# The low part of a weight sum, by VectorE's subtraction or by a DMA that adds onto the negated high part

## The chip, the cores and the metric

The kernel runs on one core of a Trainium2 chip. The core has TensorE for matrix products (PE in the profile, its weight loads PEld), VectorE (DVE) and ScalarE (ACT) for elementwise work, GpSimd (POOL) and SyncE (SP). Each engine runs its own queue of instructions in order and waits on semaphores for the others. In the kernel before, all DMAs are issued from SP's queue. The metric is the device time of one execution in microseconds, the median over runs.

## The reference, cut to what matters

The model is a trunk of two layers, each of four sublayers on 512 tokens of 1024 features: a feed-forward block, a mixer (DeltaNet in the first layer, a state-space mixer in the second), cross-attention on a memory, and a second feed-forward block. There are thus four feed-forward blocks. Each is

```python
def swiglu(x, w_in, w_out):
    gate, up = jnp.split(x @ w_in, 2, axis=-1)
    return (jax.nn.silu(gate) * up) @ w_out

u = swiglu(rms_norm(h, g[0, 0]), ffn_w_in[l, 0], ffn_w_out[l, 0])
h = h + MACARON_W * rms_norm(u, g[0, 1])
```

with 1024 features in, 2816 hidden features (22 blocks of 128) and float32 throughout.

## The kernel before

**Two parts.** TensorE is given its operands as float32r, a rounded float32. To keep the accuracy, each operand is held as a high part (the value rounded, by a ScalarE copy into a float32r tile) and a low part (value minus high part, by a VectorE subtraction). A product then takes three matmuls, high by high, high by low and low by high; `mm3` (L141 to L145) issues them, L143, L144 and L145 in the profile. `weights` (L117) loads a tile of 128 x 1024 weights from HBM into `raw` and makes the two parts at L129 and L130; `split` (L133) does the same for a tile that is in SBUF already, high part at L137, low part at L138. The parts come from two rings, `whi` and `wlo`, of five buffers each, which the weights of all products share; `raw` has three buffers.

**The feed-forward stage.** The class FFN runs through the 22 hidden blocks; for each, one tile of gate weights g and one of up weights u is loaded. Blocks 0 and 1 are done by `plain`, the other 20 by `pair`, which replaces eight products of halves by seven (halves of the tokens, of the rows, and gate and up). For that it needs four sums of weight halves, made by VectorE at L485 to L489, a and b being the two halves of 512 columns:

```python
        sub(T1, u[:, a], g[:, a])
        sub(T2, u[:, b], T1)
        sub(T4, T2, g[:, b])
        w14 = t.split(self.T14)
        sub(T3, u[:, b], u[:, a])
        w23 = t.split(self.T23)
```

T1 and T4 are the halves of the tile T14, T2 and T3 those of T23. Each of the two tiles has one buffer only, in the place of the residual stream h, which lies in DRAM meanwhile; the profile calls them `h`. So T1 of the next pair may be written only when the split of T14 of this pair has read it, and T2 and T3 of the next pair only after the split of T23.

The seven products of a pair go to PSUM in the order of the code: two of g (tile `X`), one of T23's first half (`V`, the bank called ps_f), one of the second half of u itself, whose parts are made at L492 and L493 (`Z`, against S4), two of T14 (`Y`), one of T23's second half (`Z`, against S3). S2, S3 and S4 are sums of quarters of the normalised rows, made when the stage is entered. L502 to L513 combine the results, apply SiLU and put the hidden block into two parts (L468, L469).

After most pairs follows a slice of the output products (`slices`, PSUM banks s and c): the hidden blocks done so far against one tile of output weights. `rest` issues one after pair n when enough hidden blocks are there; by its list there is none after pairs 5, 7 and 9.

**Order.** The order of the instructions on each engine is laid out ahead of the run, by a priority that follows the order of the code, by what is ready, and by offsets in the table LATER. Semaphores and the reuse of buffers follow from what each instruction reads and writes. An instruction waits in its engine's queue and holds up all behind it.

Of the kernel before, what the change touches and what calls it, by code (L numbers as in the profile page):

```python
# [61 lines left out]
class Trunk:  # L62
# [39 lines left out]
    @contextmanager  # L102
    def later(self, n):
        """what is traced here gives way to the next n instructions"""
        n = LATER.get(n, 0)
        self.tc.cur_priority += n
        yield
        self.tc.cur_priority -= n
# [4 lines left out]
    def bank(self, tag):  # L113
        """a PSUM bank: a for the long products, f, s and c for the mixers' chains"""
        return self.pm.tile([P, T], F32, name="ps_" + tag, tag=tag, bufs={"a": 3, "f": 1}.get(tag, 2))

    def weights(self, src, pool=None, nt=4):  # L117
        """a tile of weights in two float32r parts that add up to it"""
        nc = self.nc
        n = src.shape[1]  # L120
        raw = self.wp.tile([P, D], F32, name="raw", tag="raw", bufs=3)
        if pool is None:
            hi = self.wp.tile([P, D], F32R, name="whi", tag="whi", bufs=5)
            lo = self.wp.tile([P, D], F32R, name="wlo", tag="wlo", bufs=5)
        else:
            hi = pool.tile([P, D], F32R, name="thi", tag="thi", bufs=nt)
            lo = pool.tile([P, D], F32R, name="tlo", tag="tlo", bufs=nt)
        nc.sync.dma_start(out=raw[:, :n], in_=src)
        nc.scalar.copy(hi[:, :n], raw[:, :n])  # L129
        nc.vector.tensor_sub(lo[:, :n], raw[:, :n], hi[:, :n])  # L130
        return hi, lo

    def split(self, raw):  # L133
# [5 lines left out]
        return hi, lo  # L139

    def mm3(self, ps, lhs, rhs, first, last):  # L141
        mm = self.nc.tensor.matmul
        mm(ps, lhs[0], rhs[0], start=first, stop=False)  # L143
        mm(ps, lhs[0], rhs[1], start=False, stop=False)  # L144
        mm(ps, lhs[1], rhs[0], start=False, stop=last)  # L145
# [6 lines left out]
    def heads(self, srcs, half, st, outer=False):  # L152
        """the first products of a phase, for half of the tokens, block by block of the rows as they come"""
        if half == 0:
            st["w"] = [self.weights(x) for x in srcs]
            st["ps"] = [self.bank(x) for x in "aaaf"]
        s = slice(half * 256, half * 256 + 256)
        n = range(len(srcs))
        with self.later(0 if half else 'head'):
            for k, i in [(k, i) for i in n for k in range(KB)] if outer else [(k, i) for k in range(KB) for i in n]:  # L160
                kk = slice(k * P, k * P + P)
                w, ps = st["w"][i], st["ps"][i]
                self.mm3(ps[:, s], (w[0][:, kk], w[1][:, kk]), (self.xh[:, k, s], self.xl[:, k, s]),
                         k == 0, k == KB - 1)

    def out_weights(self, src, fh, pool=None, nt=4):
        """[[hi, lo] of each block of 128 rows] for 512 output columns"""
        res = []
        for kp in range(src.shape[1]):
            hi, lo = self.weights(src[fh, kp], pool, nt)  # L170
            for n in range(2):
                ns = slice(n * T, n * T + T)
                res.append((hi[:, ns], lo[:, ns]))
        return res

    def out(self, xs, ws, i, fh, first, last, tag):
        """u[tokens of tile i, columns of half fh] (+)= xs^T ws"""
        ps = self.bank(tag)
# [19 lines left out]
    def rcol(self, ss):  # L198
        """(mean of the squares + eps) ** -0.5, from the two sums of 512 squares"""
        nc = self.nc  # L200
# [6 lines left out]
    def warm(self, func, x):  # L207
        """the tables of func, loaded when x is there"""
        w = self.nt.tile([P, 1], F32, name="warm")
        self.nc.scalar.activation(w, x, func)  # L210
# [8 lines left out]
    def post(self, i, square):  # L219
        """h += u * rsqrt(mean(u^2) + eps) * gain, and the sums of the squares of h"""  # L220
        nc = self.nc
# [13 lines left out]
    def features(self, src, ss, g, hi, lo, ts, tag="c"):  # L235
        """the normalised rows of src [tokens, 1024], transposed, times gain g, in two parts"""
        nc = self.nc
# [29 lines left out]
    def last_group(self, name, og, inner, ctx):  # L267
        """the last rows of a mixer's output projection, for the tail"""
        inner.close()
        pool = ctx.enter_context(self.tc.tile_pool(name="tw", bufs=2, reuse_waits="tile"))  # L270
        return [og[12 + k] for k in range(4)], self.tail_weights(self.ap[name][3], pool, 2)
# [9 lines left out]
    def conv(self, ps, dst, w):  # L281
        """causal taps along the tokens"""
        nc = self.nc
# [5 lines left out]
    def small_proj(self, name, pool, tag, bufs):  # L289
        """the 32 columns of per-head values, [32, tokens]"""  # L290
        nc = self.nc
# [9 lines left out]
    def rsqrt(self, pool, x, shape):  # L301
        """(x) ** -0.5 elementwise by Newton steps on a float32 guess; x is a small [P, n] view."""
        nc = self.nc
# [11 lines left out]
    def softplus(self, pool, x, shape):  # L315
        """log1p(exp(x)) in place, as max(x, 0) + 2 atanh(e / (e + 2)) with e = exp(-|x|)."""
        nc = self.nc
# [17 lines left out]
class FFN:  # L335
    """the input projection by seven products of halves (of the tokens, of the rows, gate and up) for eight"""
    spill = True
# [20 lines left out]
    def sums(self):  # L358
        """place for three sums of quarters of the normalised rows, in two parts"""
        self.sp = ExitStack()  # L360
# [5 lines left out]
    def enter(self, i, ss, tag):  # L366
        """the normalised rows of tile i, and for the later half of the tokens the sums of quarters, in two parts"""
        t, nc = self.t, self.t.nc
# [37 lines left out]
    def product(self, ps, w, x, first=True, last=True):  # L406
        """ps[feature, token] (+)= w^T x over four blocks of rows"""
        for k in range(4):
# [3 lines left out]
    def early(self, n, ws, tags):  # L412
        """the first half of the tokens of a pair, by plain products"""
        ps = []
# [30 lines left out]
    def plain(self, n):  # L445
        """a pair of hidden blocks by eight products; the later half of the tokens from the sums of its quarters"""
        t, nc = self.t, self.t.nc
# [25 lines left out]
    def pair(self, n):  # L473
# [13 lines left out]
        sub(T4, T2, g[:, b])  # L487
        w14 = t.split(self.T14)
        sub(T3, u[:, b], u[:, a])  # L489
        w23 = t.split(self.T23)  # L490
        b22 = [self.ip.tile([P, T], F32R, name="b" + x) for x in "hl"]
# [24 lines left out]
    def slices(self, gi):  # L516
        """the output products of a group of hidden blocks, two blocks at a time"""
        t, nc = self.t, self.t.nc
# [41 lines left out]
class DeltaNet:  # L560
# [29 lines left out]
    def rows(self, d):  # L590
        """[row][head, chunk][column] of the 8 matrices of a pair of heads in DRAM"""
        return d.rearrange("(e x) -> e x", e=8)[:, 0:P * P].rearrange("e (i j) -> i e j", j=P)

    def diag(self, d):
        """[head, chunk, block][row][column] of their diagonal blocks"""
        return bass.AP(d.tensor, d.offset, [[self.EC // 8, 64], [P, BS], [1, BS]])
# [18 lines left out]
    def gates(self):  # L615
        """beta, the decays' sums and what the state needs of them, per token and head."""
        t, nc, d1 = self.t, self.t.nc, self.d1
# [104 lines left out]
    def blocks(self, p):  # L722
        """the diagonal blocks of 16 of I + A inverted, by substitution, a block per partition"""
        nc = self.t.nc
# [13 lines left out]
    def solve(self, p, st):  # L738
        """U = transpose of (I + A)^-1, by doubling the diagonal blocks that are inverted."""
        t, nc, dp = self.t, self.t.nc, self.dp  # L740
# [424 lines left out]
class CrossAttention:  # L1165
# [21 lines left out]
    def memory(self):  # L1187
        """the normalised memory, in the place of half of the tokens"""
        t, nc, l = self.t, self.t.nc, self.l
# [10 lines left out]
    def keys_values(self):  # L1200
        """keys [feature, slot] and values [slot, feature] of the normalised memory, to DRAM."""
        t, nc, l = self.t, self.t.nc, self.l
# [105 lines left out]
def pack_out(w, sizes):  # L1308
    """per group of row blocks: [column half][pair of row blocks][128][2 * 512]"""
    res, k0 = [], 0  # L1310
# [11 lines left out]
def pack_z(w):  # L1322
    """[1024, 2048] -> per group of 256 columns two tiles of four row blocks"""
    return np.ascontiguousarray(w.reshape(2, 4, P, 8, 256).transpose(3, 0, 2, 1, 4)).reshape(8, 2, P, 1024)
# [113 lines left out]
```

## Time and profile before

| | us |
|---|---|
| median of 3 runs | 2842.75 |
| lowest and highest | 2831.45, 2849.64 |
| span of the profiled execution | 2839.1 |

The span goes from the first to the last instruction of one profiled execution; that execution's own device time is not among the three runs, which are others. The mean granted TensorE clock in it is 0.993 of full speed.

How to read the lines that the prediction shows: a line of groups gives the line of the code, the engine, the operation, output and input by the tiles' names, the shape and the count; behind the first bar the busy time in all and the mean of one in ns, behind the second the idle time of the engine just before and what ended it. A line of a stretch gives its bounds, its length, and for each engine the busy time with the number of instructions, then the granted clock, the busy share of the DMA engines and GB/s. A line of the timeline gives start and duration of an instruction in us. A line of DMA issues gives the count, the size of one and the median time from issue to landing.

The four feed-forward stages lie at about 0 to 350, 1100 to 1480, 1480 to 1840 and 2450 to 2839 us; their loops over the hidden blocks are the four stretches in the prediction.

### The profile page before, as it was taken

What the parts mean: (1) busy time and instruction counts of PE and PEld (TensorE: products, weight loads), DVE (VectorE), ACT (ScalarE), POOL (GpSimd) and SP (SyncE); (2) the same over time, 40 slices, a digit from 0 to 9 for tenths busy, and PEclk for the clock granted to TensorE, in tenths of its full rate; (3) what the DMA queues carried; (4) which work ended last, traced back from release to release, by engine and by line L of the source; (5) the groups of instructions that cost most, each with busy time, mean ns of one, the idle gap of its engine ahead of it and who ended that gap; (6) DMA issues with size and microseconds to landing.
All of it is one profiled execution on the core that took longest, in us unless ns stands there. A gap on an engine that the chain in (4) does not pass through costs nothing.

```text
span 2839.1 us, 46420 instructions
## 1 busy us (share of the span) xinstructions
PE 2791.8 (98%) x18032; PEld 2476.0 (87%) x18032; DVE 2076.1 (73%) x4057; ACT 1520.4 (54%) x2835; POOL 128.6 (5%) x141
## 2 busy tenths in 40 slices
PE   8999999999999999999999999999999999999998
PEld 7999987788878887999988999888888888799997
DVE  8887777666666565887778877777766766588776
ACT  5444486756475574544355443575554656454433
POOL 0000001000000000000000000012221200000000
PEclk9999999999999999999999999999999999999999
DMA  6333433232323532332343333433233363233233
GB/s 222 98 105 109 154 120 94 62 106 77 92 77 115 177 113 81 127 112 90 112 149 127 98 104 97 146 118 104 91 97 111 100 211 117 77 113 112 90 111 104
DMA packets 125916, 320.76 MB, mean 113 GB/s; under 512 B 27472, under 2 KB 46672, under 8 KB 125184
## 3 DMA queue, kind: packets, MB, share of 16 engines
q1 hardware_dynamic: 125696, 317.80, 34.9%
q8 instruction: 142, 2.33, 0.3%
q14 instruction: 78, 0.64, 0.1%
HBM read 293.01 MB, written 24.74 MB: 112 GB/s over the span
## 4 chain that ended last, share of the span: by engine, by line
PE 86%; DVE 8%; ACT 2%; DMA 2%; issue 1%; POOL 0%; SPq 0%; DVEq 0%; ACTq 0%
PE ps_a L143 15%; PE ps_a L144 15%; PE ps_a L145 15%; PE ps_s L144 4%; PE ps_s L145 4%; PE ps_s L143 4%; PE ps_c L145 2%; PE ps_c L143 2%; PE ps_c L144 2%; PE ps_f L145 2%; PE ps_f L144 2%; PE ps_f L143 2%; DVE h L286 1%; PE ps_s L1243 1%; PE ps_c L1068 1%
## 5 line engine op out<-in xcount | busy, mean ns | idle before, releaser
L143 PE MATMUL ps_a<-xh,whi 128*128 128x256 f32 (+1 forms) x2368 | 754.3, 321 | 2.0 <-ACT xh L381 1.7
L144 PE MATMUL ps_a<-xl,whi 128*128 128x256 f32 (+1 forms) x2368 | 754.6, 320 | 0.1
L145 PE MATMUL ps_a<-xh,wlo 128*128 128x256 f32 (+1 forms) x2368 | 752.1, 319 | 0.0
L143 PEld LDWEIGHTS ps_a<-xh,whi 128*128 128x128 f32 x2368 | 453.2, 192 | 30.4 <-ACT xh L381 2.6
L144 PEld LDWEIGHTS ps_a<-xl,whi 128*128 128x128 f32 x2368 | 454.8, 192 | 26.3 <-DVE xl L382 0.5
L145 PEld LDWEIGHTS ps_a<-xh,wlo 128*128 128x128 f32 x2368 | 454.4, 192 | 23.6
L130 DVE TENSOR_TENSOR wlo<-raw,whi 128x1024 fp32r<-128x1024 f32 x278 | 340.3, 1226 | 167.0 <-ACT whi L129 166.7
L129 ACT CAST whi<-raw 128x1024 fp32r<-128x1024 f32 x278 | 289.0, 1043 | 214.2 <-PE ps_a L144 142.0
L137 ACT CAST whi<-h 128x1024 fp32r<-128x1024 f32 x168 | 175.6, 1048 | 209.5 <-PE ps_a L144 156.5
L138 DVE TENSOR_TENSOR wlo<-h,whi 128x1024 fp32r<-128x1024 f32 x168 | 205.4, 1224 | 89.9 <-ACT whi L137 88.7
L144 PE MATMUL ps_s<-wlo,hhi 128*128 128x512 f32 x352 | 138.0, 392 | 0.0
L143 PE MATMUL ps_s<-whi,hhi 128*128 128x512 f32 x352 | 137.8, 392 | 0.0
L145 PE MATMUL ps_s<-whi,hlo 128*128 128x512 f32 x352 | 137.2, 390 | 0.0
L492 ACT CAST bh<-raw 128x512 fp32r<-128x512 f32 x80 | 49.7, 621 | 162.9 <-DMA raw<-ffn_in 135.4
L143 PE MATMUL ps_c<-whi,hhi 128*128 128x512 f32 x288 | 112.0, 389 | 0.0
L144 PE MATMUL ps_c<-wlo,hhi 128*128 128x512 f32 x288 | 112.0, 389 | 0.0
L145 PE MATMUL ps_c<-whi,hlo 128*128 128x512 f32 x288 | 112.0, 389 | 0.0
L137 ACT CAST whi<-raw 128x1024 fp32r<-128x1024 f32 x80 | 84.0, 1050 | 51.9 <-PE ps_c L145 40.8
L138 DVE TENSOR_TENSOR wlo<-raw,whi 128x1024 fp32r<-128x1024 f32 x80 | 97.6, 1220 | 9.5 <-ACT whi L137 9.4
L485 DVE TENSOR_TENSOR h<-raw 128x512 f32<-128x512 f32 x80 | 55.1, 689 | 63.9 <-DMA raw<-ffn_in 61.7
L512 ACT ACTIVATE h<-h 128x512 f32<-128x512 f32 x80 | 50.6, 633 | 81.8 <-DVE h L509 81.5
L468 ACT CAST hhi<-h 128x512 fp32r<-128x512 f32 x88 | 54.7, 622 | 70.8 <-DVE h L513 42.7
(429 smaller groups left out, 6808.2 us busy)
## 6 DMA issues: line engine op xcount, KB each, us to landing
raw<-ffn_in SPq DMA_DIRECT2D x192, 512.0 KB, 3.9
raw<-ffn_out SPq DMA_DIRECT2D x88, 512.0 KB, 3.5
raw<-dn_in SPq DMA_DIRECT2D x48, 512.0 KB, 3.6
raw<-ssd_in SPq DMA_DIRECT2D x32, 512.0 KB, 3.6
hd<-h SPq DMA_DIRECT2D x24, 512.0 KB, 3.1
h<-hd SPq DMA_DIRECT2D x24, 512.0 KB, 4.7
raw<-dn_out SPq DMA_DIRECT2D x16, 512.0 KB, 3.6
raw<-xa_k SPq DMA_DIRECT2D x16, 512.0 KB, 3.8
```

The costliest lines, as they stand in the source:

```text
L129: nc.scalar.copy(hi[:, :n], raw[:, :n])
L130: nc.vector.tensor_sub(lo[:, :n], raw[:, :n], hi[:, :n])
L137: nc.scalar.copy(hi, raw)
L138: nc.vector.tensor_sub(lo, raw, hi)
L143: mm(ps, lhs[0], rhs[0], start=first, stop=False)
L144: mm(ps, lhs[0], rhs[1], start=False, stop=False)
L145: mm(ps, lhs[1], rhs[0], start=False, stop=last)
L286: nc.vector.scalar_tensor_tensor(dst[:, j:], ps[:, 0:T - j], w[:, 3 - j:4 - j], dst[:, j:], op0=ALU.mult, op1=ALU.add)
L468: self.t.nc.scalar.copy(hi, x)
L485: sub(T1, u[:, a], g[:, a])
L492: nc.scalar.copy(b22[0], u[:, b])
L512: nc.scalar.activation(gt, gt, AF.Silu)
```

## The change

In `pair`, the two calls of `split` for T14 and T23 become calls of a new function. The high part is made as before. The low part's tile is first filled by ScalarE with the negated value, rounded to float32r, which is the negated high part; then a DMA issued from GpSimd's queue adds the value onto it. `split` itself stays for the weights that `plain` and `pair` use directly and for the sums of `plain`. The rest of the diff takes out comment strings.

```diff
+    def split_by_dma(self, x):
+
+        nc = self.nc
+        hi = self.wp.tile([P, D], F32R, name="whi", tag="whi", bufs=5)
+        lo = self.wp.tile([P, D], F32R, name="wlo", tag="wlo", bufs=5)
+        nc.scalar.copy(hi, x)
+        nc.scalar.mul(lo, x, -1.0)
+        nc.gpsimd.dma_start(out=lo, in_=x, accum_op=ALU.add)
+        return hi, lo
+
...
-        w14 = t.split(self.T14)
+        w14 = t.split_by_dma(self.T14)
         sub(T3, u[:, b], u[:, a])
-        w23 = t.split(self.T23)
+        w23 = t.split_by_dma(self.T23)
```

## The prediction

> **What bounds the kernel now.** The page's first part was read first, then busy times by stretch for the four feed-forward loops, which hold every instruction that the change touches, then the groups by shape for the prices, then the order of time around single pairs.
>
> ```profile
> span 2839.1 us, 46420 instructions
> ...
> PE 2791.8 (98%) x18032; PEld 2476.0 (87%) x18032; DVE 2076.1 (73%) x4057; ACT 1520.4 (54%) x2835; POOL 128.6 (5%) x141
> ```
> ```profile
> core 0: us, PE busy (x) PEld busy (x) DVE busy (x) ACT busy (x) POOL busy (x), PEclk, DMA share, GB/s
> ...
> 40.00:350.00 310.00, 310.00 (x2184) 292.10 (x2183) 246.72 (x367) 137.90 (x180) 0.96 (x1) 1.00 0.37 120
> ...
> 1145.00:1440.00 295.00, 294.13 (x2114) 278.60 (x2113) 237.44 (x357) 131.89 (x173) 0.00 (x0) 1.00 0.35 109
> ...
> 1510.00:1800.00 290.00, 290.00 (x2075) 274.86 (x2075) 231.13 (x347) 128.27 (x168) 0.00 (x0) 1.00 0.33 106
> ...
> 2500.00:2795.00 295.00, 295.00 (x2117) 279.67 (x2116) 233.72 (x349) 130.19 (x170) 0.00 (x0) 1.00 0.34 108
> ```
>
> In the four loops TensorE is busy 310.00 + 294.13 + 290.00 + 295.00 = 1189.13 of 1190.00 us at a granted clock of 1.00: 0.87 us of it is idle. VectorE is busy 237.44 of 295 us in the second loop (80%), ScalarE 131.89 (45%), POOL not at all (0.96 us in the first), the DMA engines 0.33 to 0.37. So VectorE is well loaded but ends nothing here; taking work from it can't pay where TensorE has no gap. What can change the time is whether TensorE, which takes its products in a fixed order, finds a low part not yet there.
>
> **The change part by part.** The pair of lines in `split` is replaced for T14 and T23 only: 2 tiles x 20 pairs x 4 feed-forward stages = 160 times. Their prices:
>
> ```profile
> L138 DVE TENSOR_TENSOR wlo<-h,whi 128x1024 fp32r<-128x1024 f32 x168 | 205.4, 1224 | 89.9 <-ACT whi L137 88.7
> ...
> L137 ACT CAST whi<-h 128x1024 fp32r<-128x1024 f32 x168 | 175.6, 1048 | 209.5 <-PE ps_a L144 156.5 <-DVE h L487 42.2 <-DVE wlo L138 5.1
> ```
> ```profile
> L216 ACT ACTIVATE gbc<-gbc x4: 1062/1062/1063, 27.6 to 2488.7; 128x1024 f32<-128x1024 f32 x4
> ```
> ```profile
> raw<-ffn_in SPq DMA_DIRECT2D x192, 512.0 KB, 3.9
> ...
> hd<-h SPq DMA_DIRECT2D x24, 512.0 KB, 3.1
> ...
> K<-kd SPq DMA_DIRECT2D x2, 1024.0 KB, 6.2
> ...
> V<-vd SPq DMA_DIRECT2D x2, 1024.0 KB, 5.6
> ```
> ```profile
> q1 hardware_dynamic: 125696, 317.80, 34.9%
> ```
>
> - Removed: 160 subtractions of 1.224 us, 195.8 us of VectorE (the other 8 of the 168 belong to the plain pairs and stay). Worth at most the 0.87 us of idle TensorE; I take 0.
> - Added on ScalarE: 160 multiplications of the same shape as L216, 1.062 us, 169.9 us in all or 42 us a loop on top of some 132 of 295. They lie beside TensorE, which covers them; without that cover they would be on the path in full. What counts is that each stands between the cast and the DMA. In back-to-back casts ScalarE takes 2.00 us for two (rows below), so cast and multiplication make 2.00, and four make 3.9.
> - Added: 160 adding DMAs on POOL's queue, which is empty in the loops; SP's queue issues nothing more. Each moves 524,288 bytes and must also read its destination. One pass of 160 x 0.524 MB = 83.9 MB at q1's rate (34.9% of 2839.1 us for 317.80 MB) is 262 us of all engines, or 22% of the 1190 us of the loops; two passes 44%. The share goes from about 0.35 to between 0.57 and 0.79, below full, but the weight loads will land later.
> - L, the time from the end of the multiplication to the landing, is the unknown: no run here issues a DMA from POOL or one that adds. Lower end 3.1 us, the plain 512 KB store. For two reads the nearest rows are the transfers of 1024 KB, 5.6 and 6.2. Upper end 8.8: 6.2, one more pass of 262/160 = 1.6 us if the adding moves at half rate or meets the loads, and 1.0 for POOL's issue, the size of its one instruction in the first loop. I take L = 6.2, since a transfer that reads 1024 KB is nearest to one that reads 512 KB twice, and of the two such rows the upper, because the issue isn't in them.
>
> [...]
>
> **Where the landing is late.** In every pair the first product that reads a split sum is the one into ps_f, from T23, so the second split is what TensorE waits for.
>
> ```profile
> 45.89 2.00 ACT L137 CAST whi<-h 128x1024 fp32r<-128x1024 f32 x2
> ...
> 49.57 0.28 PE L143 MATMUL ps_a<-s4h,bh 128*128 128x256 f32 x1
> 49.73 0.39 PE L145 MATMUL ps_f<-s2h,wlo 128*128 128x256 f32 x1
> ```
> ```profile
> 1159.51 2.00 ACT L137 CAST whi<-h 128x1024 fp32r<-128x1024 f32 x2
> ...
> 1166.21 0.28 PE L145 MATMUL ps_f<-s2h,wlo 128*128 128x256 f32 x1
> ...
> 1254.13 1.05 ACT L137 CAST whi<-h 128x1024 fp32r<-128x1024 f32 x1 [2.26 <-PE ps_a L144]
> ...
> 1259.35 0.68 DVE L486 TENSOR_TENSOR h<-raw,h 128x512 f32<-128x512 f32 x1
> ...
> 1261.16 0.68 DVE L487 TENSOR_TENSOR h<-h,raw 128x512 f32<-128x512 f32 x1
> ...
> 1261.95 1.05 ACT L137 CAST whi<-h 128x1024 fp32r<-128x1024 f32 x1 [1.86 <-DVE h L487]
> ...
> 1274.05 1.05 ACT L137 CAST whi<-h 128x1024 fp32r<-128x1024 f32 x1
> ...
> 1274.15 0.28 PE L145 MATMUL ps_f<-s2h,wlo 128*128 128x256 f32 x1
> ...
> 1277.97 0.69 DVE L485 TENSOR_TENSOR h<-raw 128x512 f32<-128x512 f32 x1 [0.35 <-DMA raw<-ffn_in]
> ...
> 1279.75 1.05 ACT L137 CAST whi<-h 128x1024 fp32r<-128x1024 f32 x1 [1.21 <-PE ps_a L144]
> ...
> 1289.69 0.28 PE L145 MATMUL ps_f<-s2h,wlo 128*128 128x256 f32 x1
> ...
> 2506.29 2.00 ACT L137 CAST whi<-h 128x1024 fp32r<-128x1024 f32 x2
> ...
> 2512.99 0.28 PE L145 MATMUL ps_f<-s2h,wlo 128*128 128x256 f32 x1
> ```
>
> - The 64 pairs with output products ahead of them (the code puts none after pairs 5, 7 and 9, and the first pair of a stage is a case of its own: 80 - 12 - 4). The cast of T23 starts at 1279.75, when a product of the pair before releases the buffer, and its low part is first read at 1289.69. Cast and multiplication take 2.00, so L may be 9.94 - 2.00 = 7.94. At 6.2 there is 1.7 to spare: 0 us.
> - The 12 pairs without (6, 8, 10 of each stage). T23 has one buffer, so L486 of the next pair must now wait until the DMA has read it, where it waited for a subtraction. The cast at 1254.13 lands at 1254.13 + 2.00 + L = 1256.13 + L. From L486 to the end of L487 is 1261.84 - 1259.35 = 2.49, a tenth to the cast, then cast, multiplication, cast, multiplication 3.9, and L: 1262.6 + 2L, against 1274.15. The wait is 2L - 11.5 = 0.9 us at 6.2, 12 times: 10.6 us.
> - The first pair of each stage has no lead. Stages two to four: 1159.51 + 3.9 + L against 1166.21 (last of the three: 2506.29 and 2512.99), L - 2.8 = 3.5 us, 3 times 10.5. Stage one: 45.89 + 3.9 + L = 55.99 against 49.73: 6.3 us.
> - T14 is read by a DMA too, so L485 of the next pair waits for it, and behind L485 stands all of VectorE's queue. With the cast at 1274.05 the landing is 1276.05 + 6.2 = 1282.3, against L485 at 1277.97: 4.3 us blocked. VectorE has (295 - 237.44)/19 = 3.0 us of idle time a pair and gains 2 x 1.224: 5.5 in all. So it fits, up to L = 7.4; without that cover every microsecond above it is on the path of each pair. Behind it stand the sums of the pair just ended, which the output products read a pair later. The raw buffers are released later by the same 4 us, so the loads of the next weights start later; that is covered because L485 and what follows, the first to feel it (0.35 us at 1277.97), work a pair ahead of their products.
> - POOL's queue is in order: T23's DMA stands behind T14's. They are 2 to 6 us apart, so at most a fraction of a microsecond. POOL's next own work is a MEMSET when the first loop has ended.
>
> Sum without any change of order: 0 + 10.6 + 10.5 + 6.3 = 27.4 us. But the rows at 49.57 and 49.73 show that the order can give way: there a product of the other operand b was put ahead of the one whose low part was late. Such a product block lasts 12 x 0.12 = 1.44 us and has no split sum in it. If it is moved ahead wherever the low part is late, the waits become 0, 3 x 2.1 and 4.9: 11.2 us. The two differ by what the ordering knows of the DMA's duration, which nothing here shows; I take their middle, 19 us. The span 2839.1 becomes 2858; the runs' median, 2842.75 (2831.45 to 2849.64), is 3.65 us or 0.13% above the profiled span, whose own device time isn't among the three runs, and 2842.75 + 19 = 2862.
>
> **The rivals.**
> - Hidden altogether: L is 5 or less and products that need no low part are put ahead. For it: the plain store's 3.1 us and the spare room in 64 of 80 pairs. Against: the first pairs, with L - 2.8. Time 2843 to 2851. [...]
> - Slow landing, slower than before: from L = 7.4 VectorE's queue no longer recovers, and from 7.94 each of the 64 pairs waits. At L = 8.5: 64 x 0.56 = 36, 12 x 5.5 = 66, first pairs 3 x 5.7 + 8.7 = 26: 128 us, 2971; each microsecond more costs about 64 + 24 + 4 = 92. [...] Against: the 1024 KB rows at 5.6 and 6.2.
> - Faster: VectorE's relief removes TensorE's waits. The whole page has 2839.1 - 2791.8 = 47.3 us without a matmul, and 0.87 of them in the loops; for 1% it would have to remove 28 where no subtraction is removed. At best 2842.
> - That the change doesn't do what it says is hardly possible: the negated high part plus the sum is the same difference. Only its cost is open.
>
> **How the numbers follow.** Forecast 2862, with its own range of 2851 to 2885: 0.42. Hidden: 0.25. Slow landing: 0.30. Faster: 0.03. One per cent of 2842.75 is 28.4 us, about what a measurement of this kernel can tell from no change. Above 2871.2 lie the slow landing and 0.10 of the forecast: 0.40. Below 2814.3: 0.03. Within: 0.57. The range is 2836 to 2970: below it lie the faster case and a little scatter of the hidden one, 0.09, above it the landings from about 8.5 us on, 0.11.
>
> **What would show it.** The landing time of the DMA into wlo from h in the list of issues decides: below 5 us hidden, 5 to 7.4 the forecast, above it the rival. TensorE's busy time in the loops should stay full except for some microseconds at each stage's first pair and around pairs 6, 8 and 10, there with the DMA as releaser of L145 into ps_f or of L143/L144. VectorE's busy time should fall by 196 us and ScalarE's rise by 170, with new waits of L485 and L486 for the DMA. The prediction is wrong if TensorE waits in every pair, if POOL's issue takes more than about 1.5 us, or if the order of the products turns out quite different.

## The result and the profile after

| | before | after |
|---|---|---|
| median, us | 2844.36 (4 runs, 2831.45 to 2849.64) | 2942.53 (4 runs, 2939.36 to 2946.52) |
| span of the profiled execution, us | 2839.1 | 2939.2 |

The ratio is 1.0353, with an interval of 1.0327 to 1.0378: the change costs 98 us. Past `split`, the lines of the new kernel are those of the old one plus 10: the sums T1, T2, T4 and T3 are L495, L496, L497 and L499, the two parts of b L502 and L503, the combination of a pair's results L512 to L523 (L521 is the last reader of the bank of `Z`), `mm3` L153 to L155. In `split_by_dma` the cast is L146, the multiplication L147, the DMA L148.

The page's first part, its queues and its chain, for the kernel after:

```profile
span 2939.2 us, 46913 instructions
...
PE 2825.4 (96%) x18032; PEld 2499.8 (85%) x18032; DVE 1890.6 (64%) x3897; ACT 1655.0 (56%) x2995; POOL 265.6 (9%) x301
...
q0 software_dynamic: 23040, 83.90, 15.1%
...
PE 58%; DVE 15%; DMA 15%; ACT 6%; issue 5%; POOL 0%; POOLq 0%; ACTq 0%; DVEq 0%; SPq 0%
```

VectorE lost 185.5 us of work (2076.1 to 1890.6) and ScalarE gained 134.6, less than the 169.0 us of its 160 multiplications because neighbouring rows overlap by about 0.1 us (as at 1688.89 below); and yet VectorE is now more on the chain that ended last, beside the DMA. The same line of the chain before:

```profile
PE 86%; DVE 8%; ACT 2%; DMA 2%; issue 1%; POOL 0%; SPq 0%; DVEq 0%; ACTq 0%
```

The span splits in two at once. TensorE's time without a matmul was 2839.1 - 2791.8 = 47.3 us and is now 2939.2 - 2825.4 = 113.8: 66.5 us more. Its busy time for the same 18032 matmuls is 33.6 us longer. Together 100.1, the whole difference of the spans. Where the idle time comes from stands in the waits of TensorE and of VectorE after the change (who waited, for what; us in total, times, longest):

```profile
PE ps_f L155 <- DMA wlo<-h: 49.0, 35, 3.9
PE ps_a L153 <- DVE xs L521: 17.1, 12, 1.5
...
PE ps_a L155 <- DMA wlo<-h: 1.5, 1, 1.5
```
```profile
DVE h L495 <- DMA wlo<-h: 164.1, 69, 6.3
...
DVE h L496 <- DMA wlo<-h: 37.1, 28, 2.6
```

TensorE waits for low parts, 49.0 + 1.5 us, and for VectorE to empty a PSUM bank, 17.1: 67.6 in all, the added idle time to within about 1 us. Behind the second stands VectorE itself: T1's sum, L495, waits for the DMA that reads T14, 69 times and 164.1 us. The longer busy time is mostly the granted clock, 0.984 in this execution against 0.993: 2825.4 x 0.016 - 2791.8 x 0.007 makes 26 of the 33.6 us, an estimate. It shows in the busy times of the four loops after (columns as in the prediction):

```profile
40.00:365.00 325.00, 307.91 (x2151) 288.68 (x2150) 193.31 (x317) 167.80 (x215) 35.59 (x41) 0.99 0.67 170
1160.00:1475.00 315.00, 299.62 (x2099) 282.26 (x2097) 189.31 (x315) 162.88 (x215) 32.83 (x38) 0.97 0.64 161
1550.00:1870.00 320.00, 299.17 (x2055) 281.86 (x2056) 186.53 (x308) 161.99 (x209) 33.62 (x39) 0.96 0.63 156
2580.00:2890.00 310.00, 292.97 (x2031) 275.00 (x2031) 179.93 (x300) 159.47 (x204) 34.55 (x40) 0.98 0.66 164
```

TensorE was busy 99.9% of the loops; now it is 1199.67 of 1270 us, 94.5%, at a clock of 0.96 to 0.99 where the prediction's lines have 1.00. The DMA itself is in the rows of its tile (duration on POOL: lowest, median, highest in ns):

```profile
L148 POOL DMA_DIRECT2D wlo<-h x160: 855/862/1004, 48.9 to 2884.3; - x160
...
DMA to landing us min/median/max: 4.5/5.5/8.9
```

From issue to landing it takes 5.5 us, POOL's 0.86 within it. The multiplication of the rows below that starts at 1688.89 ends at 1689.94, and POOL starts at 1690.24, 0.30 later, so L, from the end of the multiplication, is 5.8 us. That is the median over both tiles. In the 69 pairs in which L495 waited for T14's DMA, it started a median of 6.0 us after the issue, and in ten of them more than 7.1 us (L above 7.4).

**Which pairs lose.** The first products into ps_f start, in the kernel before, 15.54 us apart with output products between two pairs and 10.08 without. What the spacing of the kernel after, from the timeline, has above this is the loss of each pair in us:

| stage | pair 2 | pairs 6, 8, 10 | the other 16 |
|---|---|---|---|
| 1 | 1.7 | 3.3, 6.6, 3.2 | |
| 2 | 6.4 | 2.6, 4.5, 7.2 | |
| 3 | 4.0 | 5.4, 5.1, 5.2 | |
| 4 | 5.8 | 2.6, 6.9, 3.1 | |
| sum | 17.9 | 55.7 | 27.7 |

Together 101.3, the span's growth within a little. More than half of it lies at the twelve pairs that follow the one before without output products in between.

**One such pair.** Pairs 9 and 10 of the third stage, from the timeline after the change; a bracket at the end of a line gives the idle time of the engine before it and what ended it:

```profile
1677.43 0.62 ACT L502 CAST bh<-raw 128x512 fp32r<-128x512 f32 x1 [4.02 <-DMA raw<-ffn_in]
1677.95 1.04 ACT L146 CAST whi<-h 128x1024 fp32r<-128x1024 f32 x1
...
1680.25 0.86 POOL L148 DMA_DIRECT2D wlo<-h  x1 [5.69 <-ACT wlo L147]
1680.95 0.69 DVE L495 TENSOR_TENSOR h<-raw 128x512 f32<-128x512 f32 x1 [1.85 <-DMA wlo<-h]
...
1685.20 0.28 PE L153 MATMUL ps_f<-s2h,whi 128*128 128x256 f32 x1
...
1685.33 0.69 DVE L479 TENSOR_TENSOR hlo<-h,hhi 128x512 fp32r<-128x512 f32 x1 [0.69 <-ACT hhi L478]
1685.44 0.37 PE L155 MATMUL ps_f<-s2h,wlo 128*128 128x256 f32 x1
...
1685.94 0.68 DVE L496 TENSOR_TENSOR h<-raw,h 128x512 f32<-128x512 f32 x1
...
1688.89 1.05 ACT L147 ACTIVATE wlo<-h 128x1024 fp32r<-128x1024 f32 x1
...
1690.24 0.86 POOL L148 DMA_DIRECT2D wlo<-h  x1 [9.13 <-ACT wlo L147]
...
1695.21 0.69 DVE L495 TENSOR_TENSOR h<-raw 128x512 f32<-128x512 f32 x1 [1.07 <-DMA wlo<-h]
...
1697.68 0.39 PE L155 MATMUL ps_f<-s2h,wlo 128*128 128x256 f32 x1 [1.92 <-DMA wlo<-h]
...
1697.73 0.69 DVE L496 TENSOR_TENSOR h<-raw,h 128x512 f32<-128x512 f32 x1 [1.49 <-DMA wlo<-h]
...
1699.80 0.68 DVE L521 TENSOR_TENSOR xs<-ps_a,h 128x512 f32<-128x512 f32 x1
...
1700.63 0.55 PE L153 MATMUL ps_a<-s4h,bh 128*128 128x256 f32 x1 [1.50 <-DVE xs L521]
```

The same places in the kernel before, T23's cast of pair 9, T2's sum of pair 10 and the product of pair 9:

```profile
1613.21 1.05 ACT L137 CAST whi<-h 128x1024 fp32r<-128x1024 f32 x1 [2.26 <-PE ps_a L144]
...
1618.43 0.68 DVE L486 TENSOR_TENSOR h<-raw,h 128x512 f32<-128x512 f32 x1
...
1622.91 0.28 PE L143 MATMUL ps_f<-s2h,whi 128*128 128x256 f32 x1
```

After the change, the cast of pair 9's T23 starts at 1677.95, behind a part of b whose weights came late, and 7.25 us ahead of its product at 1685.20; before the change it led by 9.70 us. Its DMA, issued at 1680.25, has landed by 1685.44, where the low part is read without a wait. So L496, which writes the T2 of pair 10 into the same tile at 1685.94, isn't held by that DMA: its row shows no wait. It stands late because of what is ahead of it in VectorE's queue: L495, which T14's DMA held for 1.85 us, then the rest of pair 8's combination, down to L479, which waits for ScalarE. From L496 the chain of T4, casts, multiplications and two DMAs takes 11.74 us to the matmul at 1697.68, and TensorE waits 1.92 us. Meanwhile the sums for pair 11 stand in VectorE's queue ahead of the combination of pair 9: L495 is blocked for 1.07 us, L496 for 1.49, and the L521 behind them empties the bank too late, so TensorE waits another 1.50.

All twelve pairs look alike in the timeline. In each, L495 waits for T14's DMA, for 1.40 to 3.90 us; L496 waits for T23's DMA in two only, for 0.30 and 0.35 us. L496 starts 9.5 to 11.1 us before its pair's low part would be read without a wait; in the kernel before it was 14.7 or 14.8.

### The profile page after: what moved, and what is told of

Its sections match the earlier page's. It is cut to its first block, busy times and chain, and to the rows that moved or that the text cites. A ratio compares the mean times of both kernels' runs of the same rounds, so it can differ in the third digit from the quotient of the medians.

```text
span 2939.2 us, 46913 instructions
## 1 busy us (share of the span) xinstructions
PE 2825.4 (96%) x18032; PEld 2499.8 (85%) x18032; DVE 1890.6 (64%) x3897; ACT 1655.0 (56%) x2995; POOL 265.6 (9%) x301
## 3 DMA queue, kind: packets, MB, share of 16 engines
q0 software_dynamic: 23040, 83.90, 15.1%
## 4 chain that ended last, share of the span: by engine, by line
PE 58%; DVE 15%; DMA 15%; ACT 6%; issue 5%; POOL 0%; POOLq 0%; ACTq 0%; DVEq 0%; SPq 0%
DMA wlo<-h 11%; PE ps_a L153 10%; PE ps_a L154 10%; PE ps_a L155 10%; PE ps_s L154 3%; PE ps_s L155 3%; PE ps_s L153 3%; DMA raw<-ffn_in 2%; DVE wlo L130 2%; ACT wlo L147 2%; ACT whi L146 1%; PE ps_c L155 1%; PE ps_c L153 1%; PE ps_c L154 1%; DVE wlo L138 1%
## 5 line engine op out<-in xcount | busy, mean ns | idle before, releaser
L153 PE MATMUL ps_a<-xh,whi 128*128 128x256 f32 (+1 forms) x2368 | 758.5, 322 | 2.4 <-ACT xh L391 2.2
L155 PE MATMUL ps_a<-xh,wlo 128*128 128x256 f32 (+1 forms) x2368 | 755.2, 320 | 1.5 <-DMA wlo<-h 1.5
L153 PEld LDWEIGHTS ps_a<-xh,whi 128*128 128x128 f32 x2368 | 457.7, 194 | 30.8 <-ACT xh L391 3.2
L155 PEld LDWEIGHTS ps_a<-xh,wlo 128*128 128x128 f32 x2368 | 458.1, 193 | 25.4 <-DMA wlo<-h 1.7
L130 DVE TENSOR_TENSOR wlo<-raw,whi 128x1024 fp32r<-128x1024 f32 x278 | 340.7, 1227 | 161.9 <-ACT whi L129 160.9
L129 ACT CAST whi<-raw 128x1024 fp32r<-128x1024 f32 x278 | 288.2, 1040 | 165.5 <-PE ps_a L154 100.7
L148 POOL DMA_DIRECT2D wlo<-h x160 | 138.2, 864 | 1725.1 <-ACT wlo L147 1316.3
L146 ACT CAST whi<-h 128x1024 fp32r<-128x1024 f32 x160 | 167.4, 1046 | 173.9 <-DVE h L497 141.3
L147 ACT ACTIVATE wlo<-h 128x1024 fp32r<-128x1024 f32 x160 | 169.0, 1056 | 0.0
L495 DVE TENSOR_TENSOR h<-raw 128x512 f32<-128x512 f32 x80 | 55.3, 691 | 164.1 <-DMA wlo<-h 164.1
L503 DVE TENSOR_TENSOR bl<-raw,bh 128x512 fp32r<-128x512 f32 x80 | 55.1, 689 | 160.3 <-ACT bh L502 157.9
L522 ACT ACTIVATE h<-h 128x512 f32<-128x512 f32 x80 | 50.5, 632 | 169.0 <-DVE h L519 168.7
L155 PE MATMUL ps_f<-s2h,wlo 128*128 128x256 f32 x320 | 96.7, 302 | 49.2 <-DMA wlo<-h 49.0
L502 ACT CAST bh<-raw 128x512 fp32r<-128x512 f32 x80 | 49.6, 621 | 161.9 <-DMA raw<-ffn_in 143.5
L153 PE MATMUL ps_s<-whi,hhi 128*128 128x512 f32 x352 | 137.8, 391 | 0.0
L155 PE MATMUL ps_s<-whi,hlo 128*128 128x512 f32 x352 | 137.2, 390 | 0.0
L153 PE MATMUL ps_a<-s4h,bh 128*128 128x256 f32 x320 | 96.4, 301 | 17.1 <-DVE xs L521 17.1
L153 PE MATMUL ps_c<-whi,hhi 128*128 128x512 f32 x288 | 112.0, 389 | 0.0
```

Of the source, the lines that this page charges most:

```text
L146: nc.scalar.copy(hi, x)
L147: nc.scalar.mul(lo, x, -1.0)
L148: nc.gpsimd.dma_start(out=lo, in_=x, accum_op=ALU.add)
L502: nc.scalar.copy(b22[0], u[:, b])
L503: sub(b22[1], u[:, b], b22[0])
L522: nc.scalar.activation(gt, gt, AF.Silu)
```

## The experiments

Each is an edit of the kernel after the change. The times are medians, the ratios stand against the kernel before on the same chip (2837.42 us up to the copy; 2841.45 for the runs with one tile by DMA, for the first run with the sums later, and for the one with the DMA only where there is room; 2839.04 for the other three). "Loss" is the difference of the medians; the change itself has 98.

**A second buffer for T14 and T23.** It takes away the wait of the next pair's sums for the DMA; the DMAs, the multiplications and the products stay.

```diff
+        self.T14b, self.T23b = [self.ip.tile([P, D], F32, name=x, bufs=1) for x in ("t14b", "t23b")]
...
+        t14, t23 = ((self.T14, self.T23), (self.T14b, self.T23b))[n % 2]
...
-        w14 = t.split_by_dma(self.T14)
+        w14 = t.split_by_dma(t14)
...
-        w23 = t.split_by_dma(self.T23)
+        w23 = t.split_by_dma(t23)
```

> T14 and T23 get a second buffer each, used by every other pair; the adding DMAs stay. Theory H (hold): the cost comes from the one buffer being held until the DMA has read it, so that the next pair's sums wait at the head of VectorE's queue and the banks behind them come free late, and the next splits start late. Then most of the 98 us goes: 2845 to 2875, and VectorE's waits for the DMA (164 us before L495, 37 us before L496) fall to nearly nothing. Theory A (late arrival): the cost is the longer way from cast to low part in itself. Then the waits of L155 into ps_f stay near 49 us and the time stays above 2910.

2859.89 us, ratio 1.0085 (1.0062 to 1.0109): 22 of the 98 us are left. The largest wait of TensorE that is left in the loops:

```profile
PE ps_f L155 <- DMA wlo<-h: 9.6, 8, 2.2
```

The wait for the bank is gone, no sum of VectorE waits for a DMA into wlo, and pairs 6, 8 and 10 lose nothing. The DMAs take 4.8 to 5.0 us by the list of issues, half a microsecond less than in the change. What is left in the loops of the profiled execution (span 2867.5) is some 16 us, 12 of it at the first pairs. So three quarters of the loss hang on the hold of the source tile: a landing of nearly the same length costs little once no sum waits for it.

**The hold without a late low part.** The low part comes from VectorE again; the multiplication and the adding DMA are still done, onto a spare tile that nobody reads, so T14 and T23 stay held until a DMA lands.

```diff
-        nc.scalar.mul(lo, x, -1.0)
-        nc.gpsimd.dma_start(out=lo, in_=x, accum_op=ALU.add)
+        nc.vector.tensor_sub(lo, x, hi)
+        spare = self.spares.tile([P, D], F32R, name="spare", bufs=2)
+        nc.scalar.mul(spare, x, -1.0)
+        nc.gpsimd.dma_start(out=spare, in_=x, accum_op=ALU.add)
```

> The low part comes from the VectorE subtraction again, early; the multiplication and the adding DMA run as in the changed kernel, but onto a spare tile that nothing reads, so T14 and T23 are held as long and the DMA engines carry as much. Theory H: the time stays well above the kernel before, 2880 to 2950, with L495 waiting for the DMA. Theory A: within 15 us of the kernel before, 2845 to 2860.

2967.37 us, 1.0458 (1.0441 to 1.0475): slower than the change itself, though no product reads what the DMA brings. Its waits (L498 is T1's sum, L147 the subtraction, L524 the combination):

```profile
PE ps_f L157 <- DVE wlo L147: 43.2, 24, 4.8
PE ps_a L155 <- DVE xs L524: 33.4, 12, 4.7
```
```profile
DVE h L498 <- DMA spare<-h: 153.2, 48, 7.1
```

T1's sum holds up VectorE's queue for 153.2 us, nearly as in the change, and behind it stand the subtraction and the combination, for which TensorE now waits. The size of the loss, 130 us, is not that of the hold in the change: the landing is 6.5 us here by the list of issues, and VectorE keeps its subtractions (2070.6 us busy against 1890.6). The run shows that a hold costs without any late low part, not how much of the 98 us it makes. Nor does it test the prediction's average over a pair: of the 5.5 us of cover only the 3.0 are left here, and at its L of about 6.8 the prediction's rows (L485 3.92 us behind the cast) give 6.8 + 2.00 - 3.92 = 4.9 us blocked, 1.9 too much in each of 64 pairs, an estimate of some 120 us.

**The multiplication alone.** The DMA gives way to a subtraction after the multiplication, into the same tile.

```diff
-        nc.gpsimd.dma_start(out=lo, in_=x, accum_op=ALU.add)
+        nc.vector.tensor_sub(lo, x, hi)
```

> The 160 multiplications on ScalarE stay, the low part then comes from the VectorE subtraction, no DMA from GpSimd. Both theories: ScalarE's 170 us lie beside TensorE, within 10 us of the kernel before (2843 to 2855). A third theory, that ScalarE's extra work delays the casts, would give more than 20 us.

2848.6 us, 1.0038 (1.0022 to 1.0053). ScalarE's 160 further instructions cost 11 us by the medians, 6 to 15 by the interval; in the profiled execution (span 2840.3) the loops lose 1.3 us. Where the rest lies was not traced.

**A copy in place of the add.** The DMA writes and doesn't add; its queue, its size and its source are those of the change. The low part's tile then holds the whole sum, so the products are not the reference's.

```diff
-        nc.gpsimd.dma_start(out=lo, in_=x, accum_op=ALU.add)
+        nc.gpsimd.dma_start(out=lo, in_=x)
```

> The DMA from GpSimd copies the sum onto the low part's tile instead of adding: one read less per element, the same issue (the low part is then the whole value, so the products are not the reference's). If the add costs by its second read, the landing falls from 5.5 us to about 4 and most waits go (2850 to 2890). If the issue and the fixed part make up the landing, it stays above 5 us and the time near 2940.

2856.96 us, 1.0083 (1.0053 to 1.0112): a loss of 20 us. The queue and the list of issues, the rows of the tile on POOL, VectorE's wait and TensorE's:

```profile
q0 software_dynamic: 23040, 83.90, 8.1%
...
wlo<-h POOLq DMA_DIRECT2D x160, 512.0 KB, 4.0
```
```profile
L148 POOL DMA_DIRECT2D wlo<-h x160: 527/530/678, 48.3 to 2799.5; - x160
```
```profile
DVE h L495 <- DMA wlo<-h: 93.7, 36, 6.4
```
```profile
PE ps_a L153 <- DVE xs L521: 9.6, 10, 1.5
```

Landing in 4.0 instead of 5.5 us takes T1's wait from 164.1 to 93.7 us, TensorE's wait for the bank from 17.1 to 9.6 and the loss from 98 to 20. The kernel stands on the steep part: between the two, each microsecond of landing, with the traffic that goes with it, is some 50 us of loss.

**One tile by DMA, the other by VectorE.**

```diff
-        w23 = t.split_by_dma(self.T23)
+        w23 = t.split(self.T23)
```

> Only T14 takes the adding DMA; T23 is split by the VectorE subtraction. Theory H (hold, shown by the second buffers; here the question is which tile's hold): if T14's hold counts, because its next writer L495 stands early in VectorE's queue (164 us of its waits in the changed kernel), 40 to 70 us are lost: 2880 to 2910. If T23's counts, whose low part is read first, this is within 15 us of the kernel before: 2838 to 2853.

2892.37 us, 1.0188 (1.0153 to 1.0222), with T14 by DMA: a loss of 51. The waits:

```profile
PE ps_a L153 <- DVE xs L521: 23.1, 12, 3.8
PE ps_f L155 <- DVE wlo L138: 17.4, 6, 5.0
```
```profile
DVE h L495 <- DMA wlo<-h: 129.2, 62, 8.3
```

TensorE waits for VectorE alone: for the bank, and for the subtraction of T23, which stands behind the blocked L495.

```diff
-        w14 = t.split_by_dma(self.T14)
+        w14 = t.split(self.T14)
```

> Only T23 takes the adding DMA. If T23's hold and late low part count, 50 to 80 us are lost: 2890 to 2920. If T14's counts, 20 us or less: below 2860, the loss at the first pair of each stage (about 12 us with second buffers) staying in either case.

2870.01 us, 1.0103 (1.0066 to 1.0141), with T23 by DMA: a loss of 29, between the two cases that were expected. Now the sum of T2 is held, for 94.5 us, by its own DMA:

```profile
DVE h L496 <- DMA wlo<-h: 94.5, 61, 3.7
```

51 + 29 = 80 of the 98 us: the two add up to most of it. T14, whose low part TensorE hardly ever waits for, costs more than T23, whose low part is read first.

**The sums later in VectorE's queue.** If the harm is that blocked sums stand ahead of the combination, they can be put behind it: the sums of pair n after the L521 of pair n - 1.

```diff
-        sub(T1, u[:, a], g[:, a])
-        sub(T2, u[:, b], T1)
-        sub(T4, T2, g[:, b])
+        with (t.tc.issue_after(self.behind) if n > 2 else nullcontext()):
+            sub(T1, u[:, a], g[:, a])
+            sub(T2, u[:, b], T1)
+            sub(T4, T2, g[:, b])
...
-        add(c2(up), c2(Z), v.unsqueeze(1).broadcast_to([P, 2, 256]))
+        self.behind = add(c2(up), c2(Z), v.unsqueeze(1).broadcast_to([P, 2, 256])).ins
```

> Both tiles by the DMA, one buffer each, but the four sums of a pair are put behind the combination of the pair before (L521, which frees a PSUM bank) in VectorE's queue. If the hold costs by the in-order queue, so that work which needs no DMA stands behind sums that wait for one, at least half of the 98 us goes: below 2895, and TensorE no longer waits for L521. If it costs by the chain itself (landing, sums, cast, landing), the time stays near 2940 or rises.

3239.34 us, 1.1398 (1.1357 to 1.1439): far off. The edit took away the lead of a pair by which the sums run ahead of their products, so TensorE waits for low parts in most pairs (70.8 us in 56 waits at ps_f, 116.9 us in 77 at ps_a), and the run doesn't tell the theories apart. With one pair more of lead, behind the L521 of pair n - 2:

```diff
+        with (t.tc.issue_after(self.ends[n - 2]) if n > 3 else nullcontext()):
...
+        self.ends[n] = add(c2(up), c2(Z), v.unsqueeze(1).broadcast_to([P, 2, 256])).ins
```

> As the changed kernel, but in VectorE's queue the sums of a pair stand behind the combination (L521) of the pair two before, so they keep the lead of more than a pair that the first attempt took away. If the hold costs by what stands behind the waiting sums, TensorE's waits for L521 (17 us) go and with them some of the reduced clock: 2880 to 2925. If it costs by the chain from landing to sums to cast to landing, the time stays at 2935 or more.

2868.26 us, 1.0102 (1.0075 to 1.0128), a loss of 29, less than expected. Tiles and DMAs are those of the change, the landing is 5.2 us instead of 5.5; what was edited is only the place in VectorE's queue. The waits (T1's sum is L496 here, T2's L497):

```profile
PE ps_f L155 <- DMA wlo<-h: 19.4, 12, 2.9
```
```profile
DVE h L497 <- DMA wlo<-h: 60.6, 48, 4.7
DVE h L496 <- DMA wlo<-h: 19.3, 15, 4.0
```

VectorE still waits for the DMA, but for 84 us (with 4.2 at T3) instead of over 200, and no product waits for the bank. Reckoned as in the table above, the first pairs lose 13.3 us, pairs 6, 8 and 10 lose 13.6 instead of 55.7, the others 4.5 instead of 27.7. So 69 of the 98 us go with the place of the sums in VectorE's queue. Of these the shorter landing is worth an estimate of some 15 us, at the 50 us for each microsecond from the copy; the two are not separated.

**Only where there is room.** Pairs 2 and 5 to 10 go back to VectorE's subtraction, the other 13 of a stage stay with the DMA.

```diff
+        split = t.split if n in (2, 5, 6, 7, 8, 9, 10) else t.split_by_dma
-        w14 = t.split_by_dma(self.T14)
+        w14 = split(self.T14)
...
-        w23 = t.split_by_dma(self.T23)
+        w23 = split(self.T23)
```

> The pairs 2 and 5 to 10 of each stage use the VectorE subtraction, the other 13 the adding DMA. In the changed kernel's trace the pairs 2, 6, 8 and 10, three of them without output products ahead, lose about 75 us and the others about 25. If the place decides, 20 to 35 us are lost: 2857 to 2872. If the loss goes with the number of DMAs, 13/20 of it stays: near 2900.

2848.84 us, 1.0034 (1.0013 to 1.0054): a loss of 7 with 104 of the 160 DMAs. Also less than expected: the 27.7 us that the other 16 pairs of a stage lose in the change are in good part the aftermath of those seven, of which pairs 5, 7 and 9 themselves lose 1.1 us in all.

**Second buffers, and the first pair by VectorE.**

```diff
+        split = t.split if n == 2 else t.split_by_dma
-        w14 = t.split_by_dma(self.T14)
+        w14 = split(t14)
...
-        w23 = t.split_by_dma(self.T23)
+        w23 = split(t23)
```

> Second buffers for T14 and T23, and the first pair of each stage (pair 2) splits by the VectorE subtraction. Of the 22 us that the second buffers alone leave, 12 lie at that pair in the trace. If this is the late arrival where there is no lead, the time comes to within 12 us of the kernel before (2841 to 2853); if the rest is the DMA traffic or ScalarE's work, it stays near 2860.

2847.5 us, 1.0029 (1.0007 to 1.005), as expected: a loss of 8. The step from 22 to 8 is the first pairs' price, some 14 us. It stays behind the kernel before.

**The product that needs T23 put later.** The order becomes b, T14, T14, T23, T23.

```diff
-        prods = [(V[:, L], half(w23, a), self.S2), (Z[:, L], b22, self.S4), (Y[:, L], half(w14, a), self.S1),
-                 (Y[:, H], half(w14, b), self.A22), (Z[:, H], half(w23, b), self.S3)]
+        prods = [(Z[:, L], b22, self.S4), (Y[:, L], half(w14, a), self.S1), (Y[:, H], half(w14, b), self.A22),
+                 (V[:, L], half(w23, a), self.S2), (Z[:, H], half(w23, b), self.S3)]
```

> As the changed kernel, but the product that reads T23's first half comes after the products of b and T14, 4.3 us later. If the direct wait for T23's low part (49 us) is a cost of its own, it falls below 15 us and the time to 2885 to 2915. If the waits only move (to T14's low part or to the banks), the time stays above 2925.

2926.4 us, 1.031 (1.0275 to 1.0345): a loss of 87. The waits:

```profile
PE ps_a L153 <- DVE xs L521: 49.8, 23, 5.4
PE ps_a L155 <- DMA wlo<-h: 1.8, 2, 1.5
```
```profile
DVE h L495 <- DMA wlo<-h: 176.5, 65, 8.6
```

TensorE hardly waits for a low part any more, 1.8 us, and waits for the bank instead, 49.8. With the late landing covered, the blocked queue takes nearly the same time. The new order also needs the bank for the product of b 1.44 us sooner, so not all of the 49.8 us is a wait that was hidden behind the other one.

No version beats the kernel before. By this route none could by much: its loops have 0.87 us of TensorE's idle time. Not tried is the DMA traffic alone, with no hold. What it costs lies within the 22 us that the second buffers leave, of which the first pairs make some 14.

## Why the prediction was wrong

It forecast 2862 us, 19 lost; 98 were. The range, 2836 to 2970, holds the time, but by luck: its upper part was there for landings of up to 8.5 us, and the time came out there with the landing near the value taken.

- Removed work worth nothing: right. VectorE shed 185.5 us and no loop became shorter; TensorE had no gap to give.
- The multiplication: sized right, 1.056 us each against 1.062. Alone, with the subtraction kept, it costs 11 us.
- L: 5.8 us against 6.2. DMA share 0.63 to 0.67, within 0.57 to 0.79. POOL's issue 0.86 against 1.0. The unknown on which the range was built came out close to the value taken.
- **The step that failed** is T14's hold: "VectorE has (295 - 237.44)/19 = 3.0 us of idle time a pair and gains 2 x 1.224: 5.5 in all. So it fits, up to L = 7.4". The median L stayed at 5.8 and it didn't fit. Idle time averaged over the pairs of a loop was set against a wait that comes at one place of an ordered queue. By the average it should have fitted: VectorE's waits for the DMA are 206.9 us over 80 pairs (164.1 and 37.1 in the lines above, 5.7 at T3), 2.6 a pair, and VectorE stands idle for 125.69 of the 315 us of the second loop. What counts is what stands right behind L495 until the DMA lands: the combination whose L521 empties the bank of `Z` (17.1 us of TensorE's waits), and the sums that let the next pair's T23 start. The prediction named that queue and priced it at zero. Second buffers, which remove the wait, bring back 76 us; the sums moved behind the combination of two pairs before bring back 69 with the hold left in; with T14 alone by DMA, and T23's low part from VectorE, 51 us are lost. With a copy that lands 4.0 us after its issue, L some 4.3, TensorE already waits 9.6 us for the bank, so the point from which it costs lies below that, not at 7.4.
- The twelve pairs without output products: the right pairs, 55.7 us against 10.6, by another wait. The term, 2L - 11.5, had T2's sum wait for T23's DMA of the pair before. That happened in two of the twelve, for 0.30 and 0.35 us; in all twelve T1's sum ahead of it waited for T14's DMA. The chain itself was not longer than forecast: from L496 to the product the forecast's 2.49 + 0.1 + 3.9 + L make 12.3 us at 5.8, and 11.74 were measured. It started too late. So this term, too, failed by what was taken as covered in T14's.
- Part of that lateness is the loads. In the rows of pair 9, T23's cast stood behind a part of b that waited 4.02 us for its weights. The prediction saw that the raw buffers would be released later and called it covered. The waits of SyncE's queue, which issues the loads, grow for the sum T4, before and after:

```profile
SPq L440 <- DVE h L487: 72.2, 32, 5.0
```
```profile
SPq L450 <- DVE h L497: 145.5, 39, 12.0
```

With the copy, which loses 20 us, the same row has 141.6 us in 39 waits; and in all the high part of b waits for its weights hardly longer than before (143.5 us against 135.4). So the late loads by themselves don't make the loss. That they shortened the lead at pair 9 is read from the order of the timeline; no run changes the load alone.

- The first pair of each stage: 17.9 us against 16.8, which is luck. In stage one it was 1.7 instead of 6.3, in the others 5.4 instead of 3.5 on average. The 16.8 is the sum for an unchanged order, and here the order gave way, as the prediction thought it might: most of the product of b was put ahead of the late low part at these four pairs (at the twelve pairs it was not). For that the forecast had 3 x 2.1 and 4.9, 11.2 us. In the second stage:

```profile
1188.06 0.28 PE L153 MATMUL ps_a<-s4h,bh 128*128 128x256 f32 x1
...
1193.19 0.58 PE L155 MATMUL ps_f<-s2h,wlo 128*128 128x256 f32 x1 [3.89 <-DMA wlo<-h]
```

TensorE waits 3.89 us where 2.1 were forecast, and slower matmuls behind the wait (a clock of 0.50 from 1193 to 1197) bring the loss to 6.4.

- The 64 pairs with output products, priced at 0: with 16 of a stage counted, 27.7 us, most of which goes when pairs 2 and 5 to 10 are mended (7 us left in all).
- The clock was not priced: 33.6 of the 100 us are longer busy time of the matmuls, by the estimate above 26 of it the lower clock, which in the loops lies next to the waits that the last section gives.
- The rivals: the slow landing named the mechanism, VectorE's queue that no longer recovers, but tied it to L above 7.4 and to an L of 8.5 for its 128 us; 98 us were lost at a median of 5.8. Hidden is out: first pairs lose 17.9 us. Faster is out.
- The sign by which the cases were to be told apart, the landing time, was the wrong one: it fell at 5.5, in the forecast's band. The waits of L495 and L496 were forecast as well, and larger (4.3 us a pair against 201 us over 80 pairs, 2.5 a pair). TensorE's wait for L521, 17.1 us, was not forecast.

## What to carry to other kernels

Work moved from an engine to a DMA kept its source tile until the landing, here some 7.8 us from the cast's start (2.0 for cast and multiplication, 5.8 to the landing). Where the next writer of that tile stands in an ordered queue, price what is queued behind it, at its place, and not against the engine's average idle time. A second buffer, or a later place for the writer that keeps its lead, took most of the cost away here, 76 and 69 of the 98 us, and as the engine relieved was not the bound, nothing was left to gain.

## What the runs showed of the hardware

**The granted clock fell after waits of TensorE of 1.3 to 3.9 us.** In the pair shown above, TensorE waits 1.92 and 1.50 us, with ten matmuls between. Its busy time in stretches of 4 us from the first on (length, busy time with count, granted clock, DMA share, GB/s):

```profile
1696.00:1700.00 4.00, 1.46 (x10) 1.00 0.26 48
1700.00:1704.00 4.00, 3.37 (x17) 0.57 0.48 135
1704.00:1708.00 4.00, 4.00 (x35) 1.00 0.80 182
```

The mean clock falls to 0.57 for a stretch, 17 matmuls in the time of some 30, and is at full speed in the next. The same happened at 1281 us after waits of 1.37 and 1.30, at 1636 after 1.99 and 1.50, and at 1667 after 1.93 and 1.30 (clock 0.59 to 0.65 in a stretch of 4 us), and at 1577 after a single wait of 2.29 (0.66). It isn't so each time: 1.30 and 1.51 us at 112 and 115 us left the clock at 1.00, so no threshold follows from these. Cut into stretches of 4 us from their starts, the four loops have a clock below 0.95 at twelve places, each next to a wait: eleven next to one for a low part of 1.37 to 3.89 us, at seven of them with one of 1.29 to 1.50 for the bank close behind, and the twelfth at 1550 us, where the third stage is entered, after waits of 3.40 and 2.24. Their lowest clocks are 0.50 to 0.77.

**An adding DMA took the DMA engines 1.92 times as long as a copy, and its landing 1.5 us more.** The 160 adding transfers took 15.1% of 16 engines' time over 2939.2 us, 444 us of all 16, the copies 8.1% of 2854.4, 231 us, for the same 23040 packets and 83.90 MB. The landing grew from 4.0 to 5.5 us only, and POOL's issue from 0.53 to 0.86. All of this is under the kernel's other traffic.
